# The routing stage of a two-block diffusion kernel: transposes in four other PSUM banks, expert weights after the overflow branch, one context step after expert 0

## The chip, the core and the metric

One core of a Trainium2 chip runs the whole program in one launch. The metric is the device time of the program in microseconds (us), the median of its runs. TensorE (PE) multiplies matrices, VectorE (DVE) and ScalarE (ACT) do elementwise work, GpSimd (POOL) copies and issues small loads, and SyncE (SP) issues the weight loads. Each engine works through its own list of instructions in order; semaphores tie the lists together.

## What is computed

Two transformer blocks over 256 tokens of 1024 columns, with a second sequence of 256 context tokens beside the second block. The first block ends in a projection, a router and a mixture of 32 experts, of which every token uses two:

```python
def moe_ffn(u, rg_w, rg_b, re_w, re_b, w1, w3, w2):
    group_p = softmax(u @ rg_w + rg_b)
    p_star, g_star = top_k(group_p, 1)
    in_group = (u @ re_w + re_b) of group g_star
    w_top, e_top = top_k(softmax(in_group), 2)
    weights = p_star * w_top / sum(w_top)
    ...
    (silu(xblk @ w1[e]) * (xblk @ w3[e])) @ w2[e]
...
x = x + gt1 * mix            # the projection's residual
h2 = modulate(rms_norm(x, norm2_g), sh2, sc2)
x = x + gt2 * moe_ffn(h2, ...)
```

The context's layer of the second block does not depend on the first block, so the kernel lets it run beside it in small steps.

## The kernel before

**Weights.** All weights come from HBM in half chunks of 128 x 2048 values (1 MB each), loaded by SP in an order that a scheduler fixed when the kernel was built. Six buffers (pool `p16`) serve the whole program, and in the stage of the routing and the experts four more (`more_chunks(es, XB)`). The four are allocated after the first block has given its SBUF memory back, so they lie where tiles of the first block lay. SP issues the loads strictly one after the other: a load whose buffer is not free holds back all behind it. An fp32 weight is split in two parts (`split_w`: `wh` on ACT, `wl` on DVE), and every product takes three matmuls.

**The projection** (`residual_part`, twice, `i` = 0 and 1) multiplies `mx` by the two halves of `w_out`. One half is 48 matmuls into two PSUM tiles (of pool `pa`, tag `A`, four banks); DVE then multiplies each by a gate (`a`) and adds it to `x` (L1596).

**The routing.** `route_part` follows each half: it transposes four 128-column tiles of `x` in pairs (`tr_pair`), each pair into one tile of `self.ps()`. That is pool `pm`, two banks, one of which holds the logits meanwhile. ACT and DVE copy each pair to `xT`, and PE multiplies `xT` by the router's weights. `route_rows` forms the reciprocal norms (`rms_stats`) and the logits; `route` finds the two experts of each token in a chain of short DVE instructions, counts tokens per expert on PE, and leaves the largest count in `maxcnt`. Then it computes the experts' weights `wt`.

**The branch.** `overflow` reads `maxcnt` on every engine and skips a block for experts with more than 32 tokens (`tc.If(rv > 32)`). The engines join behind it.

**The experts.** `moe` takes the experts in groups: `gather` picks the tokens' rows `xn` with one-hots `oh` (matmul `pm<-oh,xn`) and modulates them to `xg`; `expert` multiplies by `w1`, `w3` (`pm<-w,xg`, 64 matmuls, four half chunks) and `w2` (`pm<-w,ex`, two half chunks).

**The context steps.** `side()` advances the generator `context_side` by one step. Step 1 multiplies by `W[0]` (96 matmuls `pf<-hh,wh` and the like), step 2 by `W[2]` (48 matmuls of 512 columns, `pf<-wh,hh`) and then stores keys and values (`kv_d<-kvc`), and later steps are attention, projection and feed-forward pieces, in PSUM pool `pf`. `side(SIDE0)` stands before the branch, one `side()` after each expert. Two half chunks belong to each of steps 1 and 2.

**The conditioning.** Loads of `ada_w` and their matmuls (`pada<-w,csil`) run as background beside the projection; the last of them ends in `adab`, four transposes `qada`, and `adac`, which the router's constants (`a`, `router`) do not wait for.

Of the kernel before, what the change touches and what calls it, by code (L numbers as in the profile page):

```python
# [11 lines left out]
F32 = mybir.dt.float32  # L12
# [3 lines left out]
ALU = mybir.AluOpType  # L16
# [4 lines left out]
P = 128  # L21
# [12 lines left out]
SIDE, SIDE0 = 1.0, 2  # L34

# columns of the packed column inputs
# [21 lines left out]
class TJob:  # L58
    """out[token, n] for both token tiles: tokens stationary, weights moving."""
# [26 lines left out]
class WJob:  # L86
    """out[column, token]: weights stationary, tokens moving."""
# [24 lines left out]
class Builder:  # L112
# [23 lines left out]
    def phase(self, es, n8, n4, n2, nx, order="1284x"):  # L136
        """tile pools of one phase, in their order in memory"""
        self.nph = getattr(self, "nph", 0) + 1
        bufs = {"1": 1, "2": n2, "8": n8, "4": n4, "x": nx, "e": N_E}
        pools = {k: es.enter_context(self.tc.tile_pool(name=f"p{k}_{self.nph}", bufs=bufs[k])) for k in order if bufs[k]}  # L140
        self.p1, self.p2, self.p8, self.p4, self.px, self.pe = (pools.get(k) for k in "1284xe")

    def more_chunks(self, es, n):
        """n more half chunks in flight for a phase, which take their share of the chunks"""
        self.p16x = es.enter_context(self.tc.tile_pool(name=f"p16_{self.nph}", bufs=n))
        self.nx = n
        es.callback(setattr, self, "p16x", None)
# [82 lines left out]
    def chunk(self, src, shape=(P, 4096)):  # L230
        """weights in halves of up to 2048 columns"""
# [11 lines left out]
    def rsqrt(self, y, x, n, gain=1.0):  # L243
        """gain / sqrt(x): from the exponent trick, a step of second and one of third order"""
# [18 lines left out]
    def silu2(self, out, x, th):  # L263
        """out = 2 silu(x), as x (1 + tanh(x/2)); th is scratch"""
# [12 lines left out]
    def lin(self, chunk, nk, n, jobs):  # L277
        """chunk [128, nk*n] holds nk tiles of K rows by n columns."""
# [35 lines left out]
    def rms_each(self, x):  # L314
        """reciprocal rms norms of the two token tiles, each as soon as its columns are there"""
# [15 lines left out]
    def tr_pair(self, src, k):  # L331
        """[tok, 2, cols] -> PSUM [128 cols, 2 (k, k+1), 256 tok]"""
        p = self.ps().rearrange("p (k t) -> p k t", k=2)
# [5 lines left out]
    def put_split(self, lhs, k, n, ps):  # L339
        """PSUM [128, n, 256] -> hi and lo"""  # L340
# [9 lines left out]
    def modulated(self, x, A, B, s="h", r=None):  # L350
        """rms norm of x [tok, 2, 1024], times A plus B per column, transposed and split"""
# [16 lines left out]
    def cond(self, cols, base=False):  # L368
        """cols [128, 2, 8] -> silu, as stationary [128, 8, 32]"""
# [7 lines left out]
    def ada_open(self, bias, row_d=None):  # L377
        """bias: DRAM [3, 128, 512], rows 32j and 32j+1 hold a group's biases; row_d: DRAM for the rows of
        vector 0 of groups 1 and 2"""
        return [bias, self.one([P, 2, 6, 8], F32, "adac", True), {}, row_d]  # L380

    def ada_steps(self, st, csil, src, groups):
        """src: DRAM [12, 128, 4096]; chunk 4g + i: two K tiles by the 2048 columns of group g"""
# [25 lines left out]
    def row_bc(self, st, sec, v, s="rowbc"):  # L409
        """section sec (0..5) of vector v as rows on all partitions: [128, 1024]"""  # L410
# [9 lines left out]
    def row_load(self, st, sec):  # L420
        """section sec of vector 0 as rows on all partitions, by way of DRAM"""
# [5 lines left out]
    def mod_cols(self, st, g, v, sec):  # L427
        """A = g*(1+scale), B = shift, for sections (sec, sec+1)"""
# [17 lines left out]
    def decay(self):  # L446
        """lg [128, 8]: log-sigmoid of the decay logits (forward heads, backward heads)"""
# [51 lines left out]
    def sin_of(self, o, p, b, f):  # L499
        """sin(f*(p+b)) with the argument brought into [-pi, pi]"""  # L500
# [12 lines left out]
    def filters(self, fin, w3, dl):  # L513
        """spectra Hc = C'(hf+hb), Hs = S'(hf-hb): [128, 2, 512] each"""
# [53 lines left out]
    def ctx_states(self, kc, vc):  # L568
        """kc [128, 2, 512], vc [128, 2, 1024] -> forward and backward states [128 d, 4, 256]"""
# [17 lines left out]
    def rope1(self, x, tab):  # L587
        """x [128 d, 4, 256] with rotary angles -> new tile"""
# [13 lines left out]
    def retention(self, q, k, v):  # L602
        """q, k [128 d, 4, 256] rotated; v [128 tok, 2, 1024] -> o in PSUM, read out by readout()"""
# [48 lines left out]
    def short_conv(self, u, i):  # L652
        """u [128 ch, 4, 256] (group i of x0, x1, v) -> convolved"""
# [51 lines left out]
    def block1_mix(self, more, side):  # L705
# [48 lines left out]
        # v of tokens and context  # L754
# [77 lines left out]
    def route_setup(self, st):  # L832
        """router weights times the modulation of its inputs, and the logits' constant part"""
# [21 lines left out]
    def route_part(self, x, xT, p, i):  # L855
        """half i of the columns of x: transposed, and their part of the logits"""
        for k in range(4 * i, 4 * i + 4, 2):
            q = self.tr_pair(x, k)
# [6 lines left out]
    def route_rows(self, x, p):  # L865
        """reciprocal norms of x, and the logits"""
# [6 lines left out]
    def route(self):  # L873
        """slot positions and weights of every token and expert"""
# [4 lines left out]
        def first(v, m, n):  # L879
            """one-hot of the first entry of v that equals its maximum m"""  # L880
            q, w = self.sm([P, 2, n]), self.sm([P, 2])
# [8 lines left out]
        gm = self.sm([P, 2])  # L890
        red(gm, gl, ALU.max)
        ohg = first(gl, gm, 4)
# [4 lines left out]
        m1, m2 = self.sm([P, 2]), self.sm([P, 2])  # L897
        red(m1, ig, ALU.max)
        oh1 = first(ig, m1, 8)
# [3 lines left out]
        oh2 = first(ig2, m2, 8)  # L903
# [22 lines left out]
        nc.vector.tensor_copy(self.maxcnt, mx)  # L926
        gs, ge = self.sm([P, 2]), self.sm([P, 2, 4])
        self.tt(ge, gl, gm.unsqueeze(2).to_broadcast([P, 2, 4]), ALU.subtract)
        self.act(ge, ge, AF.Exp)
        red(gs, ge, ALU.add)  # L930
        nc.vector.reciprocal(gs, gs)
# [4 lines left out]
        nc.vector.reciprocal(w1, w1)  # L936
# [6 lines left out]
        spread(self.wt, ww)  # L943

    def gather(self, xn, A, B, e0, n):
        """slots of n experts from e0: one-hots and modulated rows [128 d, 8, 32 n]"""
# [22 lines left out]
    def scatter_mat(self, oh, e, i):  # L969
        """four times over: one-hots of expert e's slots by token [4 x 32 slots, 256 tokens], and the slots' weights"""  # L970
# [50 lines left out]
    def route_all(self, x, side, more):  # L1021
        """positions and weights of every token and expert, and the experts with more than 32 tokens"""
        self.p_keep = self.p1
        xn = self.t8([P, 2, 1024], F32, "xn")
        with self.tc.tile_pool(name="over", bufs=1) as self.p1:
# [6 lines left out]
            self.overflow(x, xn)  # L1032
        return xn, self.A2, self.B2

    def moe(self, x, side, xn, A, B):
        """x += gate * experts"""
# [3 lines left out]
        def put(e, p):  # L1040
            """y of an expert, weighted and added: the column blocks stay on their partitions"""
# [12 lines left out]
        for n in GROUPS:  # L1054
            oh, xg = self.gather(xn, A, B, e, n)
            for i in range(n):
# [6 lines left out]
                side()  # L1063
# [3 lines left out]
    def gate4(self, st):  # L1067
        """gate rows by column block: partitions 32j.. hold columns 256j.."""
# [9 lines left out]
    def gained_sum(self, x, acc, name):  # L1078
        """x = u = gained sums; returns r with u r the gained rms norm of the sums, and r' with u r' its rms norm"""
# [21 lines left out]
    def overflow(self, x, xn):  # L1101
        """tokens beyond 32 of an expert: that expert over all tokens, weighted by their share"""
# [3 lines left out]
        with tc.If(rv > 32):  # L1106
            h, y = tile_(512, "oh").rearrange("p (f t) -> p f t", f=4), tile_(256, "oy")
            wm, wc = tile_(64, "om").rearrange("p (t e) -> p t e", t=2), tile_(1, "oc")
            hT = tile_(1024, "ox").rearrange("p (k t) -> p k t", k=8)
            self.ts(wm, self.pos, 31.5, None, ALU.is_gt)  # L1110
            self.tt(wm, wm, self.wt, ALU.mult)
# [35 lines left out]
    def setup2(self, es):  # L1147
        """constants of the second block"""
# [17 lines left out]
    def lams(self):  # L1166
        """-lambda of each layer, on all partitions"""
# [15 lines left out]
    def fourier(self, A, put):  # L1183
        """A [tok, 2, 256] -> columns 0, 1"""
# [11 lines left out]
    def gelu(self, x, shape):  # L1196
        """tanh form; x is an SBUF tile, result in place"""
# [8 lines left out]
    def sgu_v(self, v, l):  # L1206
        """v [tok, 2, 256] raw -> gelu, layer norm"""
# [16 lines left out]
    def sgu(self, u, v, l, put):  # L1224
        """u [ch, 2, 256 tok] raw, v [tok, 2, 256] normed -> columns 4, 5"""
# [18 lines left out]
    def na_bias(self, l):  # L1244
        """[128 q, 2 q tiles, 4 key rows, 4 heads, 64 key columns], masked to the window;
        q columns run backwards within each row"""
# [716 lines left out]
```

## Time and profile before

| | us |
|---|---|
| median of 3 runs (lowest, highest) | 1811.08 (1808.36, 1813.09) |
| profiled execution, first to last instruction | 1809.1 |
| PE busy | 1675.7 (93%) |
| DVE / ACT / POOL busy | 982.5 / 723.0 / 97.1 |

The page shows the profiled execution by its span alone; the median of the runs lies 2.0 us above that span. The routing stage runs from about 421 us to 466 us of it, the experts from there to about 1080 us.

### The profile page before, as it was taken

How to read it: one execution, taken by the hardware profiler on the slowest of the kernel's cores; microseconds unless marked ns; L12 is line 12 of the kernel's file. 1: busy time of each engine (PE TensorE's matmuls, PEld its weight loads, DVE VectorE, ACT ScalarE, POOL GpSimd, SP SyncE). 2: the span in 40 equal slices, each digit the busy share in tenths (PEclk: the TensorE clock that was granted, in tenths of full speed). 3: DMA queues.
4: the chain of work that ended last, by engine and by line, in shares of the span. 5: the costliest groups of instructions: out<-in, count | busy, mean ns of one | idle time of the engine just before them, and what ended most of it. 6: DMA issues, size and time to landing. Idle time of an engine off the chain costs nothing.

```text
span 1809.1 us, 29140 instructions
## 1 busy us (share of the span) xinstructions
PE 1675.7 (93%) x11876; PEld 1262.9 (70%) x11876; DVE 982.5 (54%) x1747; ACT 723.0 (40%) x1246; POOL 97.1 (5%) x127
## 2 busy tenths in 40 slices
PE   5999999999888989999899989998999989979997
PEld 1678766668565556776676658775899768659996
DVE  5625556466224345454454457586655567755555
ACT  2413434343323333332232236463444445635443
POOL 0000000000000000000000002011000021110001
PEclk9899999998999999999999999999999999989998
DMA  9654678985799999899979997617555676235550
GB/s 372 265 210 163 229 268 314 345 314 211 298 420 420 405 396 369 335 422 420 399 304 422 406 378 226 213 66 285 210 192 190 232 229 204 98 111 190 191 189 35
DMA packets 79035, 495.18 MB, mean 274 GB/s; under 512 B 9024, under 2 KB 15840, under 8 KB 22832
## 3 DMA queue, kind: packets, MB, share of 16 engines
q1 hardware_dynamic: 73920, 475.94, 68.7%
q0 software_dynamic: 4000, 13.13, 2.8%
q10 hardware_dynamic: 976, 4.19, 0.6%
q8 instruction: 95, 1.56, 0.3%
q14 instruction: 44, 0.36, 0.1%
HBM read 487.43 MB, written 5.80 MB: 273 GB/s over the span
## 4 chain that ended last, share of the span: by engine, by line
PE 64%; DVE 4%; DMA 3%; issue 2%; ACT 2%; SPq 0%; ACTq 0%; DVEq 0%
PE pf L200 23%; PE pm L200 19%; PE acc L200 11%; PE pa L200 5%; PE pj L200 2%; PE pm L203 2%; DMA w<-in_w_in 1%; PE pf L203 1%; PE pada L200 1%; DMA w<-in_e 1%; DVE xn L213 0%; DVE x L1596 0%; DVE wl L273 0%; ACT eh L206 0%; DVE rq L218 0%
## 5 line engine op out<-in xcount | busy, mean ns | idle before, releaser
L206 ACT ACTIVATE wh<-w 128x1024 fp32r<-128x1024 f32 x350 | 367.2, 1057 | 399.8 <-PE pa L200 152.3
L273 DVE TENSOR_TENSOR wl<-w,wh 128x1024 fp32r<-128x1024 f32 x246 | 301.7, 1229 | 302.9 <-PE pa L200 100.3
L200 PE MATMUL pf<-hh,wh 128*128 128x256 f32 x592 | 168.4, 286 | 3.7 <-ACT wh L206 2.6
L200 PE MATMUL pf<-hl,wh 128*128 128x256 f32 x592 | 166.5, 283 | 0.0
L200 PE MATMUL pf<-hh,wl 128*128 128x256 f32 x592 | 165.1, 285 | 0.8 <-DVE wl L273 0.8
L209 DVE TENSOR_TENSOR wl<-w,wh 128x1024 fp32r<-128x1024 f32 x96 | 117.2, 1224 | 83.5 <-ACT a L206 29.5
L200 PE MATMUL pm<-w,xg 128*32 128x256 f32 x2048 | 133.0, 382 | 1.9 <-DMA w<-in_e 1.3
L200 PEld LDWEIGHTS pf<-hh,wh 128*128 128x128 f32 x592 | 113.2, 191 | 10.0 <-issue 4.1
L200 PEld LDWEIGHTS pf<-hh,wl 128*128 128x128 f32 x592 | 111.4, 191 | 3.7 <-DVE wl L273 1.2
L200 PEld LDWEIGHTS pf<-hl,wh 128*128 128x128 f32 x592 | 113.1, 191 | 1.0 <-issue 0.4
L200 PE MATMUL acc<-wl,hh 128*128 128x512 f32 x256 | 101.8, 398 | 0.0
L200 PE MATMUL acc<-wh,hl 128*128 128x512 f32 x256 | 101.3, 396 | 0.0
L200 PEld LDWEIGHTS pm<-w,xg 128*32 128x32 f32 x2048 | 64.8, 109 | 51.9 <-issue 11.9
L200 PE MATMUL pada<-w,csil 128*32 128x512 f32 x576 | 92.2, 621 | 5.0 <-DMA w<-in_ada_w 5.0
L200 PE MATMUL acc<-wh,hh 128*128 128x512 f32 x256 | 90.7, 396 | 0.0
L200 PE MATMUL pm<-w,ex 128*32 128x256 f32 x1024 | 65.2, 393 | 25.8 <-issue 24.1
L200 PE MATMUL pm<-hh,wh 128*128 128x256 f32 x256 | 72.4, 283 | 0.0
L200 PE MATMUL pm<-hl,wh 128*128 128x256 f32 x256 | 72.2, 282 | 0.0
L200 PE MATMUL pm<-hh,wl 128*128 128x256 f32 x256 | 72.0, 281 | 0.0
L200 PEld LDWEIGHTS pm<-w,ex 128*32 128x32 f32 x1024 | 34.9, 112 | 47.5 <-issue 31.4
L200 PE MATMUL pf<-wl,hh 128*128 128x512 f32 x160 | 65.3, 408 | 1.0 <-DVE wl L209 1.0
L200 PE MATMUL pf<-wh,hl 128*128 128x512 f32 x160 | 63.2, 395 | 0.0
(500 smaller groups left out, 3487.9 us busy)
## 6 DMA issues: line engine op xcount, KB each, us to landing
w<-in_e SPq DMA_DIRECT2D x192, 1024.0 KB, 10.6
w<-in_ff SPq DMA_DIRECT2D x96, 1024.0 KB, 5.0
w<-in_ada_w SPq DMA_DIRECT2D x72, 1024.0 KB, 6.9
w<-in_w_in SPq DMA_DIRECT2D x54, 1024.0 KB, 8.3
w<-in_w_out SPq DMA_DIRECT2D x16, 1024.0 KB, 7.4
w<-in_ret_w_o SPq DMA_DIRECT2D x4, 1024.0 KB, 4.9
w<-in_w_su SPq DMA_DIRECT2D x3, 1024.0 KB, 4.9
adab<-in_ada_b SPq DMA_DIRECT2D x9, 256.0 KB, 12.7
```

Of the source, the lines that this page charges most:

```text
L200: self.nc.tensor.matmul(out, lhsT, rhs, start=start, stop=stop, skip_group_check=True)
L203: self.nc.tensor.transpose(out, in_, self.ident)
L206: self.nc.scalar.activation(out, in_, f, **k)
L209: self.nc.vector.tensor_tensor(out, a, b, op=op)
L273: (self.nc.gpsimd if self.slow > 0 else self.nc.vector).tensor_tensor(lo[:, :w], src, hi[:, :w], op=ALU.subtract)
```

## The change

Three edits. The transposes of `x` in `route_part` go to `ps_lin()`, that is to the four banks of pool `pa` which the projection's own sums use, in turn with them. The computation of the experts' weights leaves `route` and becomes `route_weights`, called after `overflow`, and once more inside the skipped block; what it needs of `route` is kept in two small tiles. `SIDE0` goes from 2 to 1, and expert 0 is followed by two context steps in place of one.

```diff
-SIDE, SIDE0 = 1.0, 2
+SIDE, SIDE0 = 1.0, 1
-    def tr_pair(self, src, k):
-        p = self.ps().rearrange("p (k t) -> p k t", k=2)
+    def tr_pair(self, src, k, p=None):
+        p = (self.ps() if p is None else p).rearrange("p (k t) -> p k t", k=2)
...
         for k in range(4 * i, 4 * i + 4, 2):
-            q = self.tr_pair(x, k)
+            q = self.tr_pair(x, k, self.ps_lin())
...
-        gm = self.sm([P, 2])
+        sel, tops = self.keep([P, 2, 20], F32, "sel"), self.keep([P, 6], F32, "tops")
+        gm, m1, m2 = (tops[:, 2 * i:2 * i + 2] for i in range(3))
...
         nc.vector.tensor_copy(self.maxcnt, mx)
+        self.tops = gm, m1, m2, ohg, oh1, oh2
+    def route_weights(self, wt):
+        gm, m1, m2, ohg, oh1, oh2 = self.tops
+        gl = self.logits[:, :, 0:4]
         gs, ge = self.sm([P, 2]), self.sm([P, 2, 4])
...
             side(SIDE0)
             for _ in range(NM):
                 next(more)
             self.overflow(x, xn)
+        self.route_weights(self.wt)
         return xn, self.A2, self.B2
...
-                side()
+                side(SIDE if e else 2 * SIDE)
...
+            wo = tile_(64, "ow").rearrange("p (t e) -> p t e", t=2)
+            self.route_weights(wo)
             self.ts(wm, self.pos, 31.5, None, ALU.is_gt)
-            self.tt(wm, wm, self.wt, ALU.mult)
+            self.tt(wm, wm, wo, ALU.mult)
```

The scheduler builds new lists from this. Three places matter below.

PE at the seam between the two halves of the projection: the last two matmuls of half 0 go to `pa_2905`, those of half 1 to `pa_3014` and `pa_3015`. Before:

```order
L200 MATMUL pa_2905<-wl_2955,mxh_2760 128x512
L200 MATMUL pa_2905<-wh_2954,mxl_2761 128x512
L200 MATMUL pa_3014<-wh_3016,mxh_2760 128x512
L200 MATMUL pa_3015<-wh_3016,mxh_2760 128x512
L200 MATMUL pa_3014<-wl_3017,mxh_2760 128x512
```

and now:

```order
L200 MATMUL pa_2905<-wl_2955,mxh_2760 128x512
L200 MATMUL pa_2905<-wh_2954,mxl_2761 128x512
L200 MATMUL pada_2747<-w_3100,csil_92 32x512 x4
L203 MATMUL qada_3111<-ident_81,adab_2745 128x128 x4
L200 MATMUL pm_2893<-a_523_2890,sm_2894 128x36
L203 MATMUL pa_2988<-ident_81,x_83 128x128
L203 MATMUL pa_2999<-ident_81,x_83 128x128
L200 MATMUL pa_3014<-wh_3016,mxh_2760 128x512
```

The last conditioning matmuls, their transposes, the router's constant and the first two transposes of `x` have moved ahead of half 1; six more transposes and the first eight rows of `pm<-router,xT` now stand inside it.

DVE at the same seam: `a_540` and `a_541` are the gated sums of half 0. Before, the two splits `wl_3049` and `wl_3065` of half 1 stood ahead of all of this:

```order
L273 TENSOR_TENSOR wl_3033<-w_3010,wh_3032 128x1024
L273 TENSOR_TENSOR wl_3049<-w_3012,wh_3048 128x1024
L273 TENSOR_TENSOR wl_3065<-w_3012,wh_3064 128x1024
L209 TENSOR_TENSOR a_522_2888<-router,adac_130 128x288
L209 TENSOR_TENSOR adab_2745<-pada_2747,adab_2745 128x512
L843 TENSOR_REDUCE a_523_2890<-a_522_2888 128x36
L209 TENSOR_TENSOR router<-router,A_521_2886 128x288
L209 TENSOR_TENSOR a_540_2970<-pa_2904,rowbc_2790 128x512
```

and now:

```order
L273 TENSOR_TENSOR wl_3033<-w_3010,wh_3032 128x1024
L209 TENSOR_TENSOR adab_2745<-pada_2747,adab_2745 128x512
L209 TENSOR_TENSOR a_522_2888<-router,adac_130 128x288
L843 TENSOR_REDUCE a_523_2890<-a_522_2888 128x36
L209 TENSOR_TENSOR router<-router,A_521_2886 128x288
L209 TENSOR_TENSOR a_540_2970<-pa_2904,rowbc_2790 128x512
L209 TENSOR_TENSOR a_541_2973<-pa_2905,rowbc_2790 128x512
L209 TENSOR_TENSOR router<-router,pm_2893 128x36
L1606 TENSOR_TENSOR x_83<-x_83,a_540_2970 128x512
L1606 TENSOR_TENSOR x_83<-x_83,a_541_2973 128x512
L273 TENSOR_TENSOR wl_3049<-w_3012,wh_3048 128x1024
```

The gated sums, and the two additions to `x` that the transposes need, follow `adab`, and `adab` follows PE's last `pada`.

SP's loads around the branch: `w_3286` to `w_3411` are the four half chunks of steps 1 and 2, `w_3941` to `w_3951` expert 0, `w_4077` to `w_4081` expert 1. Before:

```order
L221 DMA w_3949<-in_e 128x2048
L221 DMA adab_11773<-in_ada_b 128x512
L221 DMA w_3951<-in_e 128x2048
L221 DMA w_3286<-in_w_in 128x2048
L221 DMA w_3409<-in_w_in 128x2048
L221 DMA w_3943<-in_e 128x2048
L221 DMA w_3947<-in_e 128x2048
L221 DMA w_4077<-in_e 128x2048
L221 DMA w_4079<-in_e 128x2048
L221 DMA w_4081<-in_e 128x2048
L1105 TENSOR_LOAD maxcnt
```

and now, where `w_3261` is the first half chunk of step 1, `w_3979` and `w_3981` are step 2, `w_3885` to `w_3895` expert 0, `w_4095` and `w_4097` expert 1:

```order
L221 DMA w_3979<-in_w_in 128x2048
L221 DMA adab_11791<-in_ada_b 128x512
L221 DMA w_3981<-in_w_in 128x2048
L221 DMA w_3261<-in_w_in 128x2048
L221 DMA w_3885<-in_e 128x2048
L221 DMA w_3891<-in_e 128x2048
L221 DMA w_3895<-in_e 128x2048
L221 DMA w_4095<-in_e 128x2048
L221 DMA w_4097<-in_e 128x2048
L1113 TENSOR_LOAD maxcnt
```

Step 2 keeps its two buffers but frees them only behind the branch, so two half chunks of expert 1 stand ahead of the branch where three stood, and the fourth, which came next before, has to wait for expert 0's buffers too.

## Rows read from the trace of the kernel before

**Rows 1.** The page: busy us (share of the span) and instructions of PE.

```profile
PE 1675.7 (93%) x11876; PEld 1262.9 (70%) x11876; DVE 982.5 (54%) x1747; ACT 723.0 (40%) x1246; POOL 97.1 (5%) x127
```

**Rows 2.** Windows: length, busy of PE, PEld, DVE, ACT, POOL, clock, DMA share, GB/s.

```profile
424.80:451.60 26.80, 25.85 (x165) 24.13 (x165) 18.50 (x65) 11.59 (x18) 2.06 (x4) 0.82 0.79 300
451.60:468.50 16.90, 14.47 (x109) 11.31 (x111) 4.87 (x13) 4.78 (x15) 1.18 (x1) 1.00 0.31 112
468.50:613.00 144.50, 127.42 (x1410) 82.53 (x1400) 49.61 (x154) 48.52 (x144) 5.46 (x11) 0.99 1.00 416
700.00:720.00 20.00, 16.30 (x151) 10.12 (x150) 14.59 (x38) 7.39 (x15) 0.40 (x1) 0.91 0.80 306
760.00:780.00 20.00, 19.99 (x206) 16.46 (x204) 9.40 (x13) 4.93 (x9) 0.40 (x1) 1.00 0.70 278
```

**Rows 3.** Chain that ended last: start, us, what.

```profile
504.78 19.76 DMA w<-in_w_in
```

**Rows 4.** Timeline of PE: start, us, tiles, shape, [idle before <-releaser].

```profile
408.59 0.63 PE L200 MATMUL pa<-wh,mxh 128*128 128x512 f32 x2
...
414.75 1.07 PE L200 MATMUL pada<-w,csil 128*32 128x512 f32 x8
...
420.75 0.40 PE L200 MATMUL pa<-wh,mxl 128*128 128x512 f32 x1
...
424.94 1.09 PE L203 MATMUL pm<-ident,x 128*128 128x128 f32 x4
...
432.28 0.56 PE L200 MATMUL pf<-hh,wh 128*128 128x256 f32 x1
...
436.34 0.98 PE L200 MATMUL pm<-router,xT 128*128 128x36 f32 x8
...
446.75 0.50 PE L200 MATMUL pf<-wh,hh 128*128 128x512 f32 x1
...
457.03 1.35 PE L200 MATMUL pm<-oh,xn 128*128 128x128 f32 x10 [1.14 <-DVE oh L209]
...
466.58 3.66 PE L200 MATMUL pm<-w,xg 128*32 128x256 f32 x64
```

**Rows 5.** Timeline of DVE, from the end of the projection to the branch.

```profile
415.35 0.65 DVE L209 TENSOR_TENSOR a<-router,adac 128x288 f32<-128x288 f32 x1
415.93 0.68 DVE L209 TENSOR_TENSOR adab<-pada,adab 128x512 f32<-128x512 f32 x1
...
417.25 1.28 DVE L209 TENSOR_TENSOR a<-pa,rowbc 128x512 f32<-128x512 f32 x2
...
418.45 1.28 DVE L1596 TENSOR_TENSOR x<-x,a 128x512 f32<-128x512 f32 x2
...
447.30 0.14 DVE L926 CAST maxcnt<-sm 128x1 int32<-128x1 f32 x1
...
451.20 0.23 DVE L209 TENSOR_TENSOR wt<-sm,sm 128x64 f32<-128x64 f32 x1
...
456.60 0.49 DVE L209 TENSOR_TENSOR oh<-router,pos 128x128 f32<-128x128 f32 x2 [5.17 <-PEq L1106]
```

**Rows 6.** What SP's issues waited for, 405 to 480 us: us, times, longest.

```profile
SPq L221 <- DVE a L306: 14.4, 1, 14.4
```

**Rows 7.** Timeline of SP's issues and of ACT.

```profile
424.87 0.80 SPq L221 DMA_DIRECT2D w<-in_w_in  x2
...
430.03 2.95 ACT L206 ACTIVATE wh<-w 128x1024 fp32r<-128x1024 f32 x3 [0.28 <-DMA w<-in_w_in]
...
468.54 0.81 SPq L221 DMA_DIRECT2D w<-in_e  x2
```

**Rows 8.** DMA, 448 to 470 us: the store's packets, MB, share.

```profile
q10 hardware_dynamic: 144, 0.79, 8.7%
```

**Rows 9.** Windows of PE: length, busy, granted clock, DMA share, GB/s.

```profile
424.00:425.00 1.00, 0.82 (x5) 0.67 0.00 0
520.00:540.00 20.00, 16.32 (x168) 0.91 1.01 420
```

More of the change, by code (lines that the diff above doesn't have):

```diff
@@ L877, in route, with first @@
         red = lambda o, v, op: nc.vector.tensor_reduce(o, v, AX.X, op)
-        def first(v, m, n):
-            q, w = self.sm([P, 2, n]), self.sm([P, 2])
+        def first(v, m, n, s):
+            q, w = s, self.sm([P, 2])
             self.tt(q, v, m.unsqueeze(2).to_broadcast([P, 2, n]), ALU.is_equal)
@@ L889, in route @@
         self.ts(self.desc, self.iota[:, :8], -1.0, 8.0, ALU.mult, ALU.add)
-        gm = self.sm([P, 2])
+        sel, tops = self.keep([P, 2, 20], F32, "sel"), self.keep([P, 6], F32, "tops")
+        gm, m1, m2 = (tops[:, 2 * i:2 * i + 2] for i in range(3))
         red(gm, gl, ALU.max)
-        ohg = first(gl, gm, 4)
+        ohg = first(gl, gm, 4, sel[:, :, :4])
         pr = self.one([P, 2, 4, 8], F32, "pr")
@@ L896, in route @@
         red(ig, pr.rearrange("p t g e -> p t e g"), ALU.add)
-        m1, m2 = self.sm([P, 2]), self.sm([P, 2])
         red(m1, ig, ALU.max)
-        oh1 = first(ig, m1, 8)
+        oh1 = first(ig, m1, 8, sel[:, :, 4:12])
         ig2 = self.sm([P, 2, 8])
@@ L902, in route @@
         red(m2, ig2, ALU.max)
-        oh2 = first(ig2, m2, 8)
+        oh2 = first(ig2, m2, 8, sel[:, :, 12:])
         both = self.sm([P, 2, 8])
@@ L929, in route @@
         self.act(ge, ge, AF.Exp)
-        red(gs, ge, ALU.add)
-        nc.vector.reciprocal(gs, gs)
+        self.nc.vector.tensor_reduce(gs, ge, AX.X, ALU.add)
+        self.nc.vector.reciprocal(gs, gs)
         e, w1, w2 = self.sm([P, 2]), self.sm([P, 2]), self.sm([P, 2])
@@ L935, in route @@
         self.ts(w1, e, 1.0, None, ALU.add)
-        nc.vector.reciprocal(w1, w1)
+        self.nc.vector.reciprocal(w1, w1)
         self.tt(w1, w1, gs, ALU.mult)
@@ L942, in route @@
         self.tt(ww, ww, w8, ALU.add)
-        spread(self.wt, ww)
+        self.tt(wt.rearrange("p t (g e) -> p t g e", g=4), ohg.unsqueeze(3).to_broadcast([P, 2, 4, 8]),
+                ww.unsqueeze(2).to_broadcast([P, 2, 4, 8]), ALU.mult)
     def gather(self, xn, A, B, e0, n):
```

## Prediction

> **What bounds the kernel now.** I read the page first: PE is busy for 93% of the span [rows 1], so the kernel is bound by TensorE wherever TensorE has its data, and the question is where it has not. Windows around the changed stage answer that [rows 2]. From 468.5 to 613 us, the first experts, the DMA share is 1.00 at 416 GB/s: the weights' loads are the limit there, a half chunk of 1.05 MB takes 2.5 us, and whatever is not yet loaded when this stretch begins is paid in it. In the two windows before it the share is 0.79 and 0.31. That is 0.21 x 26.8 + 0.69 x 16.9 = 17.3 us of idle DMA, because the buffers are full or not yet free. The chain that ended last confirms it: in the middle of that stretch it runs for 19.76 us through a single load [rows 3], from its issue to its landing. Farther on the DMA has room again: shares of 0.80 and 0.70 [rows 2].
>
> Next the timelines of the stage itself. PE's half 1 runs from 408.59 to the end of the projection at about 421.1, step 1 begins at 432.28, step 2 at 446.75, the gather at 457.03 and expert 0 at 466.58 [rows 4]. DVE's first one-hot `oh` waited 5.17 us for PE's sequencer [rows 5]: behind the branch everybody waits for PE's step 2, not for the routing's arithmetic. SP's one long wait there, 14.4 us, is for the last reader of `x` in the first block (`a`, L306) [rows 6]: step 1's first half chunk lands in memory that this scratch held. It is issued at 424.87, and `wh` of it starts at 430.03 [rows 7].
>
> **The change, part by part.** I go through it in the order of time, on the clock of the profiled execution (span 1809.1).
>
> *The transposes.* The first two stand ahead of half 1 and need `x`, so half 1 now waits for half 0's gated sums. Half 0 ends at 408.59. Ahead of them stand the 8 `pada`, 1.07 us [rows 4], to 409.7. Then DVE works through `adab`, `a`, two short ones and the two gated sums, in before 415.35 to 418.45 = 3.1 us [rows 5], a short `router` (0.15, my estimate from the short rows) and one addition to `x`, 0.6 (half of 1.28). That gives 413.6, with the semaphores some 413.75. Two transposes bring 414.0. At half clock 4 of them took 1.09 us [rows 4, 9], so I take 0.14 each at full clock. Half 1 starts 5.4 us later; about 1.9 us of this is work that before stood later (`pada`, `qada`, two transposes), and 3.5 us is a **new stall of PE**.
>
> Half 1 itself: in before the start of its last row lies 12.16 us behind its first, less 1.07 for `pada`: 11.1, or 11.3 for 48 matmuls. Six transposes (0.8) and 16 products with the router (8 took 0.98 [rows 4], so 2.0) now stand inside. It ends at 428.1, against 421.1. What was late there follows with the same distances: SP's load was issued 3.7 us behind the end of half 1, so `w_3261` is issued at 431.8, 6.9 us later than its forerunner. This first half chunk of step 1 still lies in the overlaid buffers. It lands 5.2 us behind its issue, at 437.0, and its first `wh` takes 1.0 (a third of 2.95 [rows 7]), so step 1 starts at 438.0. The logits are ready a little earlier than in before, but PE then waits for this load: **the gain of the transposes is lost behind it**.
>
> *Step 2 behind the branch.* Step 1 with the counts took 446.75 - 432.28 = 14.5 us [rows 4], of which 0.98 were products with the router that are now done before: 13.5, to 451.5. `maxcnt` follows 0.7 later (447.30 + 0.14 against 446.75 [rows 5]), the join some 0.2 after it: 452.4, where it stood at 456.5. The gather starts at 452.8, 4.2 us earlier. But it takes 25 matmuls of step 2 with it, at 0.235 = 5.9, beside its own 32 small ones (10 take 1.35 [rows 4], so 4.2), the transposes and products of the one-hot, 0.9, and two more of step 2, 0.5. Expert 0 starts at 464.3, **2.3 us earlier** than 466.58.
>
> *The weights* `wt` take DVE from 447.4 to 451.4, 4.0 us [rows 5], ahead of the branch; DVE then waited 5.17 us for PE. They move behind the branch under the gather and step 2 on PE, some 10 us. So their move is worth nothing in both directions. If that cover were gone it would cost those 4.0 us; in before, PE's step 2 covered them just as well. The small tiles that are kept cost only copies that are not there (the chain writes into them), so nothing. In the block that is skipped `route_weights` costs nothing unless an expert has over 32 tokens, which the trace does not show.
>
> *Loads and the store.* Ahead of the branch SP now issues two half chunks of expert 1 less than before had loaded by expert 0's start, because step 2's `w_3979` and `w_3981` keep their buffers until PE has done step 2. So at the moment from which the loads saturate, 2 x 2.5 = 5.0 us of loading is missing. Step 2's store of keys and values, 0.79 MB [rows 8], lay in idle DMA and now falls into the saturated stretch: 1.9 us at 416 GB/s. It is issued by ACT, on a queue of its own, so nothing queues behind it but the bandwidth. The lower bound for both is nothing (if the lag is filled later), the upper bound 6.9.
>
> The Trainium skill, page "DMA: Bandwidth & Descriptors", section "Where 436 GB/s comes from", holds that loads from HBM are limited to about 358 GB/s for a core. By that figure the missing 2.89 MB would cost 8.1 us. The trace shows 416 GB/s sustained for 144 us [rows 2], so it disagrees, and I do not use the page's figure.
>
> *The sum* is -2.3 + 5.0 + 1.9 = **+4.6 us**. A second way, on PE: at 464.3 PE still owes 21 matmuls of step 2 (4.9) and the four attention products that stood ahead of expert 0 in before (1.6, my estimate from rows of 0.4 to 0.6). That is the state before had at 466.58, reached at 470.8: 4.2 us later. Both ways agree. Span 1813.7; the median of before lies 2.0 us above the span, which I keep: **1815.7**. Its own range is 1813 to 1818, from half of the saturation's price not being paid to one more wait of two us (the last of expert 1's `w2` halves stands behind a load that waits for expert 0).
>
> **The rivals.**
>
> *The clock (slower).* At 424 to 425, after PE had waited for `x`, the granted clock was 0.67 [rows 9], on its way to 1.2 GHz. Over 424.8 to 451.6 it was 0.82 [rows 2]: 4.8 us lost, most of it under the serial transposes, where PE had to wait anyway. The change makes a stall of 3.5 us ahead of half 1, and a wait for `w_3261` ahead of step 1. If the clock falls at these places, dense matmuls on the path run at half speed. The row for 520 to 540, behind another PE wait, has 0.91 of 20 us [rows 9], 1.8 us lost. One such loss at each place is 3.6, up to the 4.8 that before lost: 1819 to 1821. Against it: before paid one of them already, and dense work brought the clock back within that window. The Trainium skill, page "TensorE: Matmul & The Clock Gate", section "HAM oscillation — how this bites in real kernels", says that waits between bursts of matmuls throttle PE again, so that each burst begins cold; the rows for 424 and 520 agree.
>
> *Absorbed (same).* The 4.6 us are taken up where the DMA has room (shares of 0.80 and 0.70 [rows 2]) or where PE waits for something that does not move. Then 1809 to 1812. For it: only one long load stands in the chain [rows 3]. Against it: at 93% PE has little slack, and work it owes does not vanish.
>
> *Faster.* Experts 15 to 20 get their context pieces in another order, since the context runs one step shifted. The DMA idles for 4.0 us from 700 to 720 and PE for 3.7, and the DMA for 6.0 us from 760 to 780 while PE is full [rows 2]. If the new order fills these, some 10 us can come back: -10 + 4.6 is -5.4 or a little better, about 1805. It decides as soon as more than the 4.6 is won there. For it: the pieces do move. Against it: PE is at 19.99 of 20 us in the second window, so only the first has PE time to give.
>
> **How the numbers follow.** What a measurement of this kernel can tell from no change is about 0.3%, or 5.4 us: 1805.7 to 1816.5. The forecast gets 0.44 (0.35 within, 0.09 above), the clock 0.26 (0.23 above, 0.03 within), absorbed 0.14 (0.12 within, 0.02 faster), the other order 0.16 (0.15 faster, 0.01 within). That makes faster 0.17, same 0.51, slower 0.32. The range reaches from the other order's 1804 to the clock's 1822.
>
> **What would show it.** In the changed profile: PE idle for some 3.5 us ahead of `pa<-ident,x`, and half 1 starting near 414; `w<-in_w_in` issued near 431.8; step 1 near 438; DVE's wait for PE ahead of `oh` shorter, with the gather near 453; expert 0 near 464; the DMA share at 1.00 from about 466, and a wait of PE for a load between 500 and 530 that is longer than before's. I am wrong if half 1 does not wait for `x`, if the load for step 1 comes no later than 426, if the clock stays below 2.4 GHz in half 1 or step 1, or if the lag at 613 is gone by 800.

## The result, and the profile after

The changed kernel takes 1822.23 us (median of 4 runs, 1820.14 to 1824.31); before 1810.26 us on the same chip. The ratio is 1.0072 (95% interval 1.0055 to 1.0088): some 12 to 13 us slower, where 4.6 were forecast and 1822 was the upper end of the range. A second series on another chip gave 1.0068 (1.0047 to 1.0089). The profiled execution has a span of 1822.5, 13.4 us above that of before.

The page of the changed kernel: PE has about the same busy time as in [rows 1] and a longer span to spread it over.

```profile
PE 1678.4 (92%) x11876; PEld 1266.2 (69%) x11876; DVE 979.1 (54%) x1747; ACT 723.2 (40%) x1246; POOL 97.6 (5%) x127
```

PE's timeline of the changed kernel in the stage (start, us, tiles, idle before and its releaser; answers to [rows 4]):

```profile
410.25 0.66 PE L203 MATMUL qada<-ident,adab 128*128 128x128 f32 x4 [0.81 <-DVE adab L209]
411.41 0.38 PE L200 MATMUL pm<-a,sm 128*128 128x36 f32 x2 [0.50 <-DVE a L843]
413.58 0.64 PE L203 MATMUL pa<-ident,x 128*128 128x128 f32 x2 [1.79 <-DVE x L1606]
413.87 0.78 PE L200 MATMUL pa<-wh,mxh 128*128 128x512 f32 x1
...
431.30 0.94 PE L203 MATMUL pa<-ident,x 128*128 128x128 f32 x4 [2.09 <-DVE x L1606]
...
438.77 0.58 PE L200 MATMUL pf<-hh,wh 128*128 128x256 f32 x1 [2.90 <-ACT wh L206]
...
457.56 5.44 PE L200 MATMUL pm<-oh,xn 128*128 128x128 f32 x32 [3.43 <-DVE oh L209]
462.76 0.48 PE L200 MATMUL pf<-wh,hh 128*128 128x512 f32 x1
...
468.96 3.66 PE L200 MATMUL pm<-w,xg 128*32 128x256 f32 x64
```

Half 1 starts at 413.87 behind a stall, step 1 at 438.77 behind another, the gather at 457.56 behind a third, and expert 0 at 468.96, 2.4 us later than before instead of 2.3 earlier. What SP's issues waited for, 405 to 480 us, and SP's timeline (a row with a long time holds the wait): the load into the overlaid buffers waits 22.5 us, where [rows 6] has 14.4. It is the second issue of its row, which ends at 409.56 + 23.40 = 432.96; a single issue takes 0.33 us there, so it goes out at 432.6, where [rows 7] has 424.87.

```profile
SPq L221 <- DVE a L306: 22.5, 1, 22.5
```

```profile
409.56 23.40 SPq L221 DMA_DIRECT2D w<-in_w_in  x2
```

Windows of PE in the changed kernel (length, busy, granted clock, DMA share, GB/s): the clock is at its lower level for part of half 1, through the first 5.5 us of step 1, and for most of the gather.

```profile
413.00:418.00 5.00, 4.42 (x14) 0.66 0.18 74
418.00:432.00 14.00, 11.81 (x64) 1.00 0.00 0
438.70:444.20 5.50, 5.40 (x23) 0.50 1.02 424
444.20:454.00 9.80, 9.80 (x85) 0.99 0.76 286
457.50:462.70 5.20, 5.13 (x31) 0.67 0.42 121
```

DVE's timeline at the branch (answers to [rows 5]): `maxcnt` is there at 450.75, the one-hot starts at 457.08, and what it waited for is PE's sequencer at the branch (PEq). `wt` follows under the gather and nothing waits for it.

```profile
450.60 0.15 DVE L926 CAST maxcnt<-sm 128x1 int32<-128x1 f32 x1
...
457.08 0.49 DVE L209 TENSOR_TENSOR oh<-router,pos 128x128 f32<-128x128 f32 x2 [3.79 <-PEq L1114]
...
460.25 0.23 DVE L209 TENSOR_TENSOR wt<-sel,sm 128x64 f32<-128x64 f32 x1
```

The instructions of the branch's line, in before and then in the changed kernel (duration in ns, start in us): PE's own compare-and-branch takes 3.7 and 3.9 us. Nothing else of that line takes over 0.1 us.

```profile
L1106 PEldq COMPARE_BRANCH  x1: 3725/3725/3725, 452.7 to 452.7; - x1
```

```profile
L1114 PEldq COMPARE_BRANCH  x1: 3867/3867/3867, 453.0 to 453.0; - x1
```

Where the 13.4 us lie, by the start of the same instruction in both traces: expert 0 is 2.4 late, expert 9's `ex` 9.95 (622.07 against 612.12), expert 31's 8.5 (1093.69 against 1085.20); another 3.2 come between there and the second block's first projection, 1.7 after it.

The stretch to the experts is read from windows of PE with the DMA behind it (length, busy, granted clock, DMA share, GB/s). Before, then the changed kernel:

```profile
400.00:432.00 32.00, 29.70 (x141) 0.88 0.52 186
432.00:440.00 8.00, 8.00 (x60) 0.84 1.01 421
440.00:460.00 20.00, 18.86 (x114) 1.00 0.40 130
460.00:474.00 14.00, 12.55 (x136) 1.00 0.61 238
474.00:600.00 126.00, 111.35 (x1240) 0.99 1.01 421
```

```profile
400.00:432.00 32.00, 26.71 (x130) 0.95 0.34 115
432.00:440.00 8.00, 4.83 (x26) 0.63 0.81 303
440.00:460.00 20.00, 16.54 (x115) 0.84 0.60 232
460.00:474.00 14.00, 14.00 (x120) 0.95 0.40 134
474.00:600.00 126.00, 112.55 (x1182) 1.00 1.01 419
```

GB/s times length gives the bytes moved. The changed kernel is 2.3 MB behind at 432, while the first load waits for `x`, and 3.2 MB at 440. By 460 that is down to 1.2 MB: before has idle DMA there (a share of 0.40), so most of the late bytes are made good. From 460 to 474 another 1.5 MB are lost, and from there both kernels load at the same rate, 421 and 419 GB/s. At 600 2.9 MB are missing, which are 6.9 us at 416 GB/s.

This full-rate stretch starts when PE comes to expert 0. SP's next load then waits for a buffer: in before for one that expert 0's first products (`pm`) free, in the changed kernel for the last split of step 2's weights (`wl`), which DVE makes when PE's step 2 lets it. What SP waited for, 462 to 472 us, in before and then in the changed kernel:

```profile
SPq L221 <- PE pm L200: 10.8, 2, 9.9
```

```profile
SPq L221 <- DVE wl L273: 10.4, 1, 10.4
```

The load goes out 1.4 us behind expert 0's first product in the changed kernel (468.96, above), 2.0 us behind it in before (466.58 in [rows 4], 468.54 in [rows 7]). In all 18 traces of this case that distance is 1.4 or 2.0 us.

```profile
470.39 1.33 SPq L221 DMA_DIRECT2D w<-in_e  x3
```

Two more things differ when it starts. Only 9 half chunks of the experts' weights have been issued in the changed kernel, against 10 in before (counted in SP's timeline). And step 2's store, which before issues at 461.61 into idle DMA, goes out at 479.60, inside the full-rate stretch. Before, then the changed kernel:

```profile
461.61 0.34 ACTq L1735 DMA_DIRECT2D kv_d<-kvc  x1
```

```profile
479.60 0.33 ACTq L1745 DMA_DIRECT2D kv_d<-kvc  x1
```

So the full rate starts 1.9 us later, one half chunk is missing (2.5 us) and the store has to be fitted in (1.9 us). These sum to 6.3 us, close to the 6.9 that the bytes show. The experts lag a little more than their loads: expert 5 is 9.5 us late, by its `ex` in before and in the changed kernel. The 2.6 us between were not traced.

```profile
548.72 0.28 DVE L218 SCALAR_TENSOR_TENSOR ex<-eth,pm 128x128 f32<-128x128 f32 x1
```

```profile
558.19 0.28 DVE L218 SCALAR_TENSOR_TENSOR ex<-eth,pm 128x128 f32<-128x128 f32 x1
```

Of the 3.2 us behind the experts 2.8 are PE's longer wait behind `nab`, a table of the second block. DVE's timeline of before and of the changed kernel, and PE's wait for the split `wl` that DVE makes next (us, times, longest):

```profile
1133.47 2.29 DVE L209 TENSOR_TENSOR nab<-nab,k 128x2048 f32<-128x2048 f32 x1 [3.62 <-DMA nab<-in_na_rpb]
```

```profile
1143.12 2.29 DVE L209 TENSOR_TENSOR nab<-nab,k 128x2048 f32<-128x2048 f32 x1 [6.34 <-DMA nab<-in_na_rpb]
```

```profile
PE pa L200 <- DVE wl L273: 2.3, 1, 2.3
```

```profile
PE pa L200 <- DVE wl L273: 5.1, 1, 5.1
```

In the changed kernel's list one split fewer stands ahead of `nab`, so PE runs dry sooner while DVE waits for the table: 5.1 us against 2.3. No line of this part was edited; the scheduler made its list anew.

### The profile page after: what moved, and what is told of

Same layout as the page of the kernel before. It is cut to its first block, busy times and chain, and to the rows that moved or that the text cites. A ratio compares the mean times of both kernels' runs of the same rounds, so it can differ in the third digit from the quotient of the medians.

```text
span 1822.5 us, 29126 instructions
## 1 busy us (share of the span) xinstructions
PE 1678.4 (92%) x11876; PEld 1266.2 (69%) x11876; DVE 979.1 (54%) x1747; ACT 723.2 (40%) x1246; POOL 97.6 (5%) x127
## 4 chain that ended last, share of the span: by engine, by line
PE 64%; DVE 4%; issue 3%; DMA 2%; ACT 2%; SPq 0%; DVEq 0%; POOL 0%; ACTq 0%
PE pf L200 23%; PE pm L200 19%; PE acc L200 11%; PE pa L200 4%; PE pj L200 2%; PE pm L203 2%; PE pf L203 1%; PE pada L200 1%; DMA nab<-in_na_rpb 1%; DMA w<-in_ff 1%; DVE x L1606 0%; DMA k_d<-planes 0%; ACT a L206 0%; DVE wl L209 0%; DVE wl L273 0%
```

## Experiments

Theory A came first: the transposes ahead of half 1 delay `x`, hence the first load, and take step 2 away from the branch. Rival B: the moved context step is the cause. "Ahead" is the number of step 2's 512-column matmuls ahead of the branch in the list. "First load" is the issue of the first load into the overlaid buffers, "expert 0" the start of its first product. MB are those moved from 408 to 613 us, GB/s times length in the windows 408 to 432, 432 to 468 and 468 to 613. All ratios are to before on the same chip.

| kernel | ratio (95%) | ahead | first load, us | expert 0, us | MB |
|---|---|---|---|---|---|
| before | | 38 | 424.9 | 466.6 | 71.5 |
| changed | 1.0072 (1.0055, 1.0088) | 0 | 432.6 | 469.0 | 67.9 |
| e1 context step only | 0.9990 (0.9976, 1.0004) | 38 | 423.9 | 462.9 | 72.9 |
| e2 transposes only | 1.0057 (1.0035, 1.0079) | 22 | 432.0 | 473.5 | 68.2 |
| e3 without context step | 1.0083 (1.0064, 1.0103) | 0 | 431.4 | 473.1 | 68.3 |
| e4 without transposes | 1.0053 (1.0036, 1.0071) | 22 | 424.9 | 466.6 | 70.8 |
| e5 before again | 0.9999 (0.9982, 1.0017) | 38 | 425.7 | 466.8 | 71.4 |
| e6 weights only | 1.0032 (1.0015, 1.0050) | 26 | 424.5 | 468.4 | 70.6 |
| e7 changed, half 1 only | 1.0002 (0.9988, 1.0015) | 0 | 425.4 | 463.2 | 71.0 |
| e8 transposes only, half 1 only | 1.0052 (1.0036, 1.0068) | 26 | 423.6 | 464.7 | 72.1 |
| e9 late load, third pair | 1.0040 (1.0027, 1.0054) | 0 | 429.4 | 473.3 | 68.5 |
| e10 late load, fourth pair | 1.0134 (1.0115, 1.0153) | 0 | 432.4 | 473.6 | 67.7 |
| e11 without the weights' move | 1.0083 (1.0062, 1.0104) | 22 | 433.0 | 472.7 | 67.8 |
| e12 changed again | 1.0068 (1.0047, 1.0089) | 0 | 433.6 | 468.5 | 68.2 |
| e13 before, second list | 1.0029 (1.0013, 1.0046) | 38 | 423.4 | 463.6 | 72.6 |
| e14 changed, second list | 1.0077 (1.0054, 1.0101) | 0 | 432.1 | 468.3 | 68.2 |
| e15 e7, second list | 1.0034 (1.0020, 1.0048) | 0 | 425.3 | 462.6 | 71.2 |
| e16 e7, third list | 1.0034 (1.0021, 1.0047) | 0 | 425.4 | 462.3 | 71.4 |

In the eight traces with a late first load expert 0 is late as well, and 67.7 to 68.5 MB are moved by 613, against 70.6 to 72.9 in the other ten. The two go together in these kernels, so the table alone does not say which of them takes the bytes.

### The parts alone and left out (e1 to e4, e6, e11)

The edits are the lines of the diff of the change, each alone on the kernel before or undone in the changed one. e1: `SIDE0` and `2 * SIDE` alone.

> The kernel before with only SIDE0 from 2 to 1 and two context steps after expert 0. In its instruction list all 38 matmuls of step 2 still stand ahead of the branch and three half chunks of expert 1 are loaded there, as before. Theory A (the transposes bring the stall and take step 2 away from the branch; the moved step by itself does nothing at the branch): expert 0 starts within 1 us of before's 466.6, and the only loss is late in the program, where nab now stands one split earlier on VectorE, as in the changed kernel: +3 to +5 us. Rival B (the moved context step is the cause): +8 us or more, expert 0's first loads late and a lag of 5 us or more at 613.

> The kernel before with only the transposes in the banks of pa. 22 matmuls of step 2 stand ahead of the branch instead of 38, two half chunks of expert 1 instead of three. Theory A: PE stalls some 5 us behind half 0, the clock falls in half 1 and in step 1, step 1 starts near 438.8 as in the changed kernel; the 22 matmuls cover PE's branch, so PE does not stand behind it; lag at 613 some 5 to 8 us, and 3 to 4 more late in the program by nab's place: +8 to +12. Rival B: no more than +3, since the context step is where it was.

> The changed kernel with SIDE0 back at 2 and one step after expert 0. No matmul of step 2 stands ahead of the branch even so, and two half chunks of expert 1 do, but late in the program one more split stands ahead of nab, as before. Theory A: the stage as in the changed kernel (expert 0 at 468 to 470, lag 8 to 10 us at 613), less the 3 to 4 us late in the program: +7 to +9. Rival B: within 3 us of before.

> The changed kernel with the transposes back in pool pm: expert weights behind the branch and the context step moved remain. 22 matmuls of step 2 ahead of the branch, three half chunks of expert 1, the split ahead of nab as before. Theory A: no stall at the seam, step 1 near 432, PE does not stand behind the branch, late part as before: within 3 us of before. Rival B: +6 us or more.

Rival B falls: the context step alone does nothing (e1), and undoing it alone gives nothing back (e3, which lost some 15 us where theory A had 7 to 9). Whether step 2 stands ahead of the branch is not set by `SIDE0` at all: the scheduler kept all 38 matmuls there in e1 and none in e3. Two parts of theory A missed. e1's late part did not show as a loss in the median, and e4, which has neither seam nor late load, still lost 0.53%. PE did wait behind the branch in e4 (2.5 us) and in e2 (1.7 us), against what I wrote: in e4 22 matmuls queued ahead did not cover 5.5 us. The branch's line and PE's wait in e4:

```profile
L1114 PEldq COMPARE_BRANCH  x1: 5525/5525/5525, 448.8 to 448.8; - x1
```

```profile
PE pf L200 <- PEq L1114: 2.5, 1, 2.5
```

> The changed kernel with the transposes in pool pm and SIDE0 at 2: only the expert weights behind the branch remain. 26 matmuls of step 2 stand ahead of the branch, 22 behind it; 38 and 10 in before. Theory A (PE's own branch takes 3.6 to 5.5 us of its sequencer in every kernel, and matmuls queued ahead must cover it): PE waits 1.5 to 3 us behind the branch, as with 22 matmuls in the kernel without the transposes; +2 to +6. Rival C (the weights' arithmetic itself is late behind the branch): PE waits for wt ahead of expert 0, at 460 to 470, and the loss is there. Rival D (nothing in the stage, only the clock elsewhere): no longer wait of PE in the stage, yet a mean clock below before's by 0.005 or more.

PE waits 2.1 us for `oh` behind the branch, as theory A has it (1.1 and 1.4 in the two traces of before); nothing waits for `wt`, so rival C falls. Rival D's clock is there too: the mean granted clock of e6's runs is 0.971, of before's on the same chip 0.976. The longer wait speaks against D, but the run does not part the two. The 0.32% are within the expected range, but e13 below gives the same without any edit to the stage.

> The changed kernel without the move of the expert weights: transposes in the banks of pa and the context step. 22 matmuls of step 2 ahead of the branch. Theory A: the load into the overlaid buffers 7 to 8 us late, +7 to +11, as the transposes alone (+0.57%), since the context step alone did nothing. Rival B (transposes and context step hurt only together with the weights): 0 to +3.

The loss is there without the weights' move, so the combination with it is not needed.

### The seam taken away (e7, e8)

```diff
-            q = self.tr_pair(x, k, self.ps_lin())
+            q = self.tr_pair(x, k, self.ps_lin() if i else None)
```

> The changed kernel with only half 1's transposes in the banks of pa, half 0's in pm as before: the two transposes no longer stand ahead of half 1. No matmul of step 2 stands ahead of the branch, two half chunks of expert 1 do, all as in the changed kernel. Theory A: no wait of PE for x at the seam (3.9 us in the changed kernel), step 1 starts some 5 us earlier than its 438.8, the wait behind the branch stays at 3 us or more: +5 to +9 against before, 3 to 6 better than the changed kernel. Rival B (the seam is hidden anyway because step 1's load sets the pace): as the changed kernel, +11 to +14.

> The kernel before with only half 1's transposes in the banks of pa, nothing else. 26 matmuls of step 2 ahead of the branch, two half chunks of expert 1. Theory A: no wait at the seam, step 1 no later than 434, PE waits 1 to 3 us behind the branch: 0 to +5. Rival (any use of these banks by the transposes costs): +8 or more, as with all transposes in them.

e7 undoes one half of one edit and is back at the time of before, more than theory A expected; rival B, which had it as slow as the changed kernel, falls. SP's timeline, PE's behind the branch and at expert 0, windows as above, and expert 5's `ex` in e7:

```profile
410.38 15.34 SPq L221 DMA_DIRECT2D w<-in_w_in  x2
```

```profile
450.50 6.76 PE L200 MATMUL pm<-oh,xn 128*128 128x128 f32 x32 [4.04 <-DVE oh L209]
...
463.21 3.66 PE L200 MATMUL pm<-w,xg 128*32 128x256 f32 x64
```

```profile
464.64 2.59 SPq L221 DMA_DIRECT2D w<-in_e  x4
```

```profile
400.00:432.00 32.00, 28.88 (x153) 0.96 0.51 180
432.00:440.00 8.00, 7.96 (x52) 0.74 1.02 423
440.00:460.00 20.00, 15.96 (x101) 0.83 0.38 132
460.00:474.00 14.00, 13.95 (x115) 1.00 0.61 235
474.00:600.00 126.00, 113.77 (x1248) 1.00 1.01 419
```

```profile
552.08 0.28 DVE L218 SCALAR_TENSOR_TENSOR ex<-eth,pm 128x128 f32<-128x128 f32 x1
```

The first load goes out at 425.4 (the end of its row less one issue of 0.33), near before's 424.9. PE stands 4.0 us behind the branch, longer than in the changed kernel; step 2 follows the gather, 9 half chunks of the experts are issued ahead of expert 0, and the store lies behind expert 0's start (473.9), all as in the changed kernel. What differs is expert 0: it starts at 463.2, 5.8 us ahead of the changed kernel and 3.4 ahead of before. The full rate starts 3.9 us ahead of before's, which pays for most of the half chunk and the store (4.4 us together): by 600 only 0.4 MB are missing, 1.0 us, where the changed kernel misses 2.9. Expert 5 is 3.4 us late against 9.5. The lists e15 and e16 repeat this (expert 0 at 462.6 and 462.3, expert 5 2.8 and 2.5 late), as e12 and e14 repeat the changed kernel (468.5 and 468.3, 9.0 and 8.9). In all six traces expert 5's lag is expert 0's plus 6.7 to 7.1 us.

From expert 7 on the lags also follow the order of the loads. e7 is 0.7 us ahead of before at expert 9 and 1.6 behind it at expert 31. e8, again without a seam, lost 0.52%: it is 7.0 us ahead of before at expert 9 and 9.5 behind it at expert 31, so its loss lies among experts 10 to 31, not in the stage. Its loss fits the rival that any use of these banks by the transposes costs; against that rival stands e7, which uses them for the same half.

### The first load made late, without the transposes (e9, e10)

```diff
+        jd = self.t2([P, 512])
+        self.nc.vector.tensor_copy(self.r2, self.rms_stats(x, (self.t2([P, 512]), jd)))
+        nc.vector.tensor_copy(jd[:, 0:1], late)      # late = xT[:, 5, 0:1] or xT[:, 7, 0:1]
```

> The kernel before, transposes where they were, with one added copy of 128 x 1 values from xT's third pair into the scratch of the norms, so that the first load into the overlaid buffers waits for it: by before's rows it is issued some 4.5 us later (430 instead of 425). Nothing else is added; the scheduler's list has no matmul of step 2 ahead of the branch, as the changed kernel. Theory A (the experts are bound by their loads, so a later first load is kept to the end of the experts): idle time of the DMA from 408 to 1080 some 4 us above before's 62 to 63, expert 31 some 3 to 5 us late, time +3 to +6. Rival E (the seam costs by PE's own stall and clock, and the load's start is hidden): 0 to +2.

> The same with the fourth pair of xT: the load is issued some 9 us later than in before (434), a little later than in the changed kernel (433). Theory A: idle time of the DMA 408 to 1080 some 8 us above before's, expert 31 some 7 to 10 us late, time +7 to +11, twice the dose of the third pair. Rival E: 0 to +3, no more than with the third pair.

SP's timeline in e9 and e10:

```profile
429.36 0.80 SPq L221 DMA_DIRECT2D w<-in_w_in  x2
```

```profile
432.38 0.80 SPq L221 DMA_DIRECT2D w<-in_w_in  x2
```

The DMA of e9 in two of the windows above:

```profile
400.00:432.00 32.00, 29.23 (x142) 0.88 0.35 123
440.00:460.00 20.00, 17.10 (x109) 0.89 0.58 215
```

Both lose more time than rival E had for them, 0.40% and 1.34%, but they do not settle it. Their lists put the whole of step 2 between the branch and expert 0, which starts at 473.3 and 473.6, 7 us late. And the late bytes themselves were made good in e9: 2.0 MB behind before at 432, some 0.3 at 460. Theory A's own signs missed on both sides. From 408 to 1080 us e9 moves 373 GB/s and before 374, which is 1.6 us of loading and not 4, and its expert 31 is 1.4 us late, not 3 to 5; e10 moves 359, its expert 31 is 27.0 us late, and it lost 24 us in all, 7.3 of them by expert 9 and 17 more by expert 16, where its list is another. No run delays the first load alone.

### The same stage on another list (e5, e12 to e16)

e13 to e16 add 2 to 16 memsets of an unused tile on DVE, which has idle time there, as

```diff
+        pad = self.tx([P, 256], F32, "pad")
+        for _ in range(2):
+            self.nc.vector.memset(pad, 0.0)
```

> The kernel before, unchanged, for a trace on the same chip as the three that follow, and for what two series of the same kernel differ by. All theories: within 2 us of before.

> The changed kernel, unchanged, on the chip of the three above, for its trace and for how far its late part (from 1085 on) repeats. All theories: +11 to +14. If the late part is chance, the time from the last expert to the second block's products, 122 us in its first trace and 113 to 119 in two traces of before, comes out differently; if it is the list, 121 to 123 again.

e12 repeats all: expert 9 is 9.5 late, PE waits 5.15 us behind `nab` again, and from the last expert to the second block it takes 122.3 us, as in the first trace (121.9). But before itself took 118.7 and 112.8 there in its two traces, with PE waiting 2.3 and 0 us, so the list is one part of it and the load of `nab` the other. That load took some 17 us in nine traces: there PE waited 2.1 to 2.3 us behind it with 11 splits ahead of `nab` (before, e3, e10) and 5.0 to 5.2 with 10 (changed, e1, e6, e9, e11, e12). So the split is worth some 2.9 us when the load is long. In the other nine traces the load took 14 to 15 us and PE waited 0 to 2.6.

> The kernel before with two added memsets of 128 x 256 values into an unused tile ahead of expert 0 on VectorE, which is idle there; they cost nothing themselves, but the scheduler makes another list behind the branch (SP's order differs in some 20 rows, VectorE's in some 280). Theory L (the list alone moves the time by 0.3 to 0.5%, either way): outside -0.2 to +0.2%. Theory A (the losses are the edits' own): within 0.2% of before.

> The changed kernel with sixteen added memsets of an unused tile behind expert 16 on VectorE; SP's order differs in some 30 rows from there on, the stage itself is unchanged. Theory A: still +0.6 to +0.8% against before, as the 8 to 10 us are lost ahead of expert 10. Theory L: anything from +0.2 to +1.2%.

> The changed kernel with only half 1's transposes in the banks of pa (1.0002 of before), and two added memsets ahead of expert 0; SP's order differs in some 10 rows, VectorE's in some 200. Theory A: within 0.2% of before again. Theory L: its zero was a lucky list, and it now lies +0.2 to +0.6%.

> The same with eight added memsets behind expert 9 instead; SP's order differs in some 18 rows, VectorE's in some 50. Theory A: within 0.2% of before. Theory L: +0.2 to +0.6%.

Both theories hold a part. The seam stays at +0.77% on another list (e14), and e15 and e16 lie at +0.34%, not at 0: e7's zero was partly a good list, and so is before's (e13, +0.29% for two memsets). Before itself repeats (e5, 0.9999).

## Why the prediction was wrong, by its own steps

**Right.** Half 1 at 414.0 (413.87), its stall of 3.5 us (0.81 + 0.50 + 1.79 = 3.1 by the waits for `adab`, `a` and `x`), the load at 431.8 (432.6), step 1 at 438.0 (438.77), the time from the gather to expert 0 (11.5 forecast, 11.4 measured), `wt` hidden, the store in the stretch at full rate. "The gain of the transposes is lost behind" the load: yes. So is the form of the sum: expert 0's start, the missing half chunks and the store are what the loads lag by.

**The step that failed: "expert 0 starts 2.3 us earlier".** It started 2.4 later, at 468.96 instead of 464.3, 4.7 off. Of these, 0.8 are step 1's later start. 1.9 are step 1's length, 15.4 us instead of 13.5 (to 454.13, the gather's start less PE's idle time): the granted clock was 0.50 for its first 5.5 us. 2.1 are PE's stand behind the branch, 3.43 us where I had 1.3. I had the clock as a rival at 0.26, and "if the clock stays below 2.4 GHz in half 1 or step 1" among the signs of being wrong; in half 1 it was 0.66 over the first 5 us. Ahead of 424, where I read the clock in before, PE had waited for `xT` (0.5 and 0.9 us) and not for `x`.

The term behind the 2.1 us is the 0.2 us that I took from `maxcnt` to the join, because I read DVE's 5.17 us in [rows 5] as waiting for PE's step 2. That is half of it. In before PE's branch begins at 452.7, 5.3 us behind `maxcnt`, with step 2's matmuls ahead of it in PE's list; then PE's own compare-and-branch takes 3.7 us, with step 2 still running under it. In the changed kernel `maxcnt` is there at 450.75, PE's branch begins at 453.0 and ends at 456.9: 6.1 us, not 0.2, and with no matmuls of step 2 queued ahead PE stood for 3.43. That this cost only 2.1 is luck: `maxcnt` came 3.4 us ahead of the end of step 1, because the counts stand inside it, and not 0.7 behind it as I had it. The wait named PE's sequencer, and the branch's line would have shown it. The Trainium skill, page "Advanced Engine Details and Errata", section "Control Flow Timing", gives some 0.1 us for a compare-and-branch; DVE, ACT, POOL and SP stay within that (0.05 to 0.07 us), PE in this program does not (3.4 to 5.5 us in all 18 traces). The Trainium skill, page "Runtime: NRT & Kernel Launch", section "Instruction fetch mechanics", says that a taken branch to code outside the pages at hand must first fetch it; that would fit, but no run here shows it as the cause.

**The term "5.0" was mis-sized.** One half chunk fewer was issued ahead of expert 0, not two: 2.5 us. The store's 1.9 stands. Expert 5's lag beyond expert 0's, 7.1 us, is near my 6.9 in part by luck, since 2.6 of it are not missing bytes.

The whole miss in the profiled executions is 13.4 against 4.6 us. Of these 8.8, 4.7 are expert 0's start. From there to expert 9 the lag grows by 7.6 where I had 6.9, 0.7 more; 1.5 are given back by expert 31, and 4.9 come behind it.

**Nothing was forecast** for the late part. The list is made anew by any edit, and that alone moved the time by 0.3% (e13), as much as the bound below which I spoke of no change. By the medians the loss divides roughly so: against e7 on three lists (1.0002, 1.0034, 1.0034) the seam in three series on two lists (1.0072, 1.0068, 1.0077) costs about 0.5%, or 9 us; the remaining 0.2% is left to the half chunk, the store and the list, which no run parts. The traces show the seam's cost up to expert 9 (expert 9 is 9.3 to 9.95 us late with it, 0.7 to 1.6 early without). They do not show where it stays: at expert 31 the lags are 6.6 to 8.5 us with it and 1.6 to 6.7 without. Why e4 and e8 lose their 0.5% was not found; the mean granted clock of their runs is lower than before's (0.969 against 0.977, 0.971 against 0.976), and no run shows whether that is the cause.

## What to carry to other kernels

Where a later stage is bound by its loads, find the event that starts its full-rate stretch, here PE's coming to expert 0, which sets buffers free, and price a move by three things: when that event comes, how many loads are out by then, and what else must be moved inside the stretch. A late first load counted here by what it did to that event; of its own bytes most were made good in the idle DMA ahead of it. Look up what a wait for a sequencer consists of before calling it a wait for the work that runs meanwhile; here 3.7 us of branch hid under matmuls. And with a scheduler that rebuilds the whole list, make two or three lists of the same edit before believing a difference of 0.3%.

## What was not expected of the hardware

PE's compare-and-branch took 3.4 to 5.5 us where the other engines' took 0.05 to 0.07. The load of `nab` took either 13.9 to 14.9 or 16.8 to 17.1 us from its first issue to its last landing, within one kernel too (14.6 and 17.0 in two traces of before), and PE's wait behind it followed: 0 to 2.6 us after the short load, 2.1 to 5.2 after the long one.
